# A decoder block on one core: first adaLN columns in two groups of 256, gates spread in one place, partial sums copied back into PSUM, another order of work

## The chip, the core and the metric

The kernel runs on one core of a Trainium2 chip. The time is device microseconds of one execution. The core has a matrix engine (TensorE, PE in the profile, with weight loads as PEld), a vector engine (VectorE, DVE), a scalar engine (ScalarE, ACT), GpSimd (POOL), and SyncE (SP), which here only issues DMAs. Each engine works through its own list of instructions in order and waits on semaphores for the others.

## What is computed

One layer of a hybrid decoder, 256 tokens of width 2048, in float32. Cut to what matters:

```python
mod = jax.nn.silu(c) @ w_ada[l] + b_ada[l]
sh1, sc1, g1, sh2, sc2, g2 = jnp.split(mod, 6, axis=-1)
h = modulate(rms_norm(x, norm1_g[l]), sh1, sc1)
proj = h @ w_in[l]
q, k, v, gb, gc, xt = jnp.split(proj, ...)
attn = moba_attention(q, k, v)
conv = gb * causal_dwconv(gc * xt, conv_w[l], conv_b[l])
mixed = jnp.concatenate([rms_norm(attn, attn_out_g[l]), rms_norm(conv, conv_out_g[l])], axis=-1)
x = x + g1[:, None, :] * (mixed @ w_out[l])
h2 = modulate(rms_norm(x, norm2_g[l]), sh2, sc2)
u = causal_dwconv(h2 @ w_ffn_up[l], ffn_conv_w[l], ffn_conv_b[l])
u_gate, u_up = jnp.split(u, 2, axis=-1)
x = x + g2[:, None, :] * ((jax.nn.silu(u_gate) * u_up) @ w_ffn_down[l])
```

`modulate(h, shift, scale)` is `h * (1 + scale) + shift`. With 256 tokens the attention has one block of keys and is plain causal attention over 8 heads of 128. Six vectors of 2048 (shift, scale and gate, twice) come out of the adaLN product of one row `c` with a matrix of 2048 by 12288.

## The kernel before

**Matrices.** Every large product splits its weights into two float32r parts, `hi` (a ScalarE copy, L640) and `lo` (the rest, a subtraction on VectorE or GpSimd, L649), and does the same with the activations. The input and output projections (`mm_tok`, L869 to L871) run three matmuls of 128x512 per block: hi by hi, lo by hi, hi by lo. A weight tile arrives as 512 KB in one of 10 buffers called `raw`; `lo` frees it and the next load is issued.

**Turns.** The program is a list of turns (slots in the code). The 49 turns of the input projection take four blocks of 128x512 each (the first three turns three, three and two); then come 16 turns of the output projection, then the FFN, up in matmuls called `z` (L1201, L1205), down in `mm_tok`. The six outputs have two halves each (q0, q1, k0 and so on); `turns` in the table CFG says which half is fed with which rows in which order. Consecutive turns of one half stay in two PSUM banks; when another half must have the banks, `evac_in` copies the sum out to SBUF (`pa_`, ScalarE, L881) or adds it there (VectorE, L883). What stands in the turn's loop is written into the engines' lists in that order: hi of the turn after next, tasks due in this turn, lo, adaLN steps, more tasks, then the matmuls of the turn.

**AdaLN.** A group is a stretch of columns of one of the six vectors. `ada` lists groups as part (0 shift 1, 1 scale 1, 2 gate 1, 3 shift 2, 4 scale 2, 5 gate 2), first block of 128, width, whether TensorE does it, first turn and span. On TensorE (L708) each 128 rows of the matrix are one matmul with 32 columns of weights, and four of them sit side by side in the array. On VectorE each 128 rows are one multiply-add with a column of `silu(c)` (L725). The numbers under `pre`, `mid` and `carry` say how many of these steps VectorE does at three places of a turn and how many it may leave. Then `evac` copies a TensorE group to SBUF, and `cols` (transposes, `adac`, and a sum, `adaz`) turns it into the columns A1 and B1 of `h = x*A1 + B1`, which `h_chunks` writes. A gate goes another way: `spread` (L786 to L799) sums the partitions with ones on TensorE into one row per quarter (`adab`), adds the bias, writes the row to DRAM, and `broadcast` reads it back to all partitions. The groups of gate 1 are spread one by one, and so are those of gate 2.

**The start** is written by hand. Blocks 0 and 1 of shift and scale are four TensorE groups of 128 columns; `x` is scaled (`xr`), transposed (`xn`) and copied out (`xnT`); turn 0 runs after block 0, turn 1 after block 1. Small vectors (`v`, `vf`: gains, conv weights) come over GpSimd's queue and are transposed into columns by `ffn_cols` (`pv_`, L575).

**The order around it.** `at` puts a task into a turn, `move` in CFG shifts a task by turns and within the turn, `pool` says per turn which of the two lo pieces go to GpSimd (1 first, 2 second, 3 both), `hi_late` whether hi comes after the first tasks.

Of the kernel before, what the change touches and what calls it, by code (L numbers as in the profile page):

```python
# [8 lines left out]
F32 = mybir.dt.float32  # L9
# [5 lines left out]
P = 128  # L15
# [16 lines left out]
CFG = {'ada': [[1, 2, 256, True, 0, 3], [0, 2, 256, True, 0, 3], [1, 4, 512, False, 2, 7], [0, 4, 512, True, 5, 4],  # L32
# [5 lines left out]
 'bufs': [41, 14, 10, 6, 2],  # L38
# [9 lines left out]
 'pre': {1: 0,  # L48
         2: 2,
         3: 0,  # L50
         4: 3,
         5: 3,
         6: 3,
         7: 2,
         9: 2,
         10: 4,
         11: 2,
         12: 2,
         13: 3,
         14: 0,  # L60
         15: 0,
         16: 2,
         17: 3,
         18: 4,
         20: 2,
         22: 0,
         23: 2,
         24: 0,
         27: 2,
         29: 0,  # L70
         30: 2,
         34: 3,
         36: 2,
         38: 2,
         39: 3,
         40: 4,
         42: 4,
         44: 0,
         46: 2,
         48: 2,  # L80
         51: 0,
         52: 3,
         54: 2,
         56: 3,
         57: 0,
         58: 2,
         61: 4,
         62: 4,
         63: 3,
         64: 3,  # L90
         65: 3,
         67: 4,
         69: 0,
         70: 0,
         74: 2,
         76: 3,
         77: 4,
         80: 0,
         83: 2,
# [4 lines left out]
         93: 0,  # L104
         95: 2,
         96: 3,
         97: 2,
         101: 2,
         103: 2,
         107: 3,  # L110
         112: 4,
         117: 3,
# [16 lines left out]
 'mid': {0: 4, 2: 4, 47: 1, 1: 4, 100: 1, 75: 0, 94: 3, 52: 0, 50: 1, 92: 4, 6: 3, 63: 0, 159: 2, 54: 0, 58: 2},  # L129
 'pool': {4: 1,  # L130
          5: 3,
          6: 3,
          9: 1,
# [8 lines left out]
          18: 3,  # L142
# [3 lines left out]
          22: 3,  # L146
          23: 3,
          24: 3,
          26: 3,
          27: 3,  # L150
          29: 3,
          31: 3,
          32: 3,
          33: 3,
          34: 3,
          35: 3,
          37: 3,
          38: 3,
          39: 3,
          2: 1,  # L160
          3: 2,
          40: 3,
          41: 1,
          48: 3,
          58: 0,
          49: 1,
# [4 lines left out]
          62: 2},  # L171
 'pool_h': [2, 3, 4, 5, 6, 7, 8, 9, 10, 11, 12, 13, 14, 15],
 'psum': [[0, 39]],
 'carry': {0: 2,
           1: 2,
           2: 2,
           4: 6,
           6: 1,
           9: 4,
           10: 3,  # L180
           12: 4,
           13: 4,
           14: 2,
           18: 4,
           21: 2,
           22: 1,
           30: 2,
           32: 6,
           34: 2,
           35: 4,  # L190
           36: 4,
           37: 4,
           38: 4,
           39: 3,
           43: 4,
           45: 6,
           46: 6,
           49: 2,
           50: 2,
           51: 3,  # L200
           52: 3,
           54: 3,
           55: 3,
           56: 3,
           57: 4,
           58: 4,
           59: 3,
           60: 4,
           61: 1,
           62: 3,  # L210
           63: 4,
           64: 4,
           65: 1,
           66: 2,
           67: 1,
           69: 3,
           72: 1,
           73: 2,
           74: 4,
           76: 2,  # L220
           79: 1,
# [22 lines left out]
           150: 2,  # L244
           159: 4,
# [1489 lines left out]
```

## Time and profile before

| what | value |
|---|---|
| median of 3 runs | 1183.02 us (1182.31 to 1183.23) |
| the profiled execution | 1182.27 us |
| its span in the trace | 1180.5 us |
| granted TensorE clock | 0.999 |
| instructions on TensorE, VectorE, ScalarE, GpSimd | 6045, 1305, 1015, 111 |
| read from HBM | 314.87 MB, 270 GB/s over the span |
| first projection matmul | 19.81 us |
| first FFN matmul | 441.83 us |
| hi pieces on ScalarE | 401 |
| lo pieces on VectorE, on GpSimd | 334, 67 |

A row of the profile names the line, the engine, the operation, the tile written and the tiles read. Matmuls overlap in the pipe, so the duration of one is longer than the distance to the next; rates are taken from the distance. Idle time of an engine counts only if the end of the program waits for it.

### The profile page before, as it was taken

Reading aid. Unit: us, or ns where it says so; the run is one execution under the profiler, and the core shown is the slowest. Engines: PE = TensorE matmul, PEld = TensorE weight load, DVE = VectorE, ACT = ScalarE, POOL = GpSimd, SP = SyncE. Lnnn points to the kernel's source line nnn. Section 1 sums busy time; section 2 is a strip of 40 time slices with the busy share of each in tenths; the row PEclk is TensorE's granted clock in tenths of the full one; section 3 lists DMA queues with packets and bytes.
Section 4 is the critical chain, followed back from the end, with each engine's and each line's share of the span. In section 5 each row is a group of like instructions: output and inputs, shape, how many; then the busy total and the mean of one; then the engine's idle time right before and its main releaser. Section 6 shows DMA issues by size and latency. Waiting matters only on the chain.

```text
span 1180.5 us, 17260 instructions
## 1 busy us (share of the span) xinstructions
PE 1156.3 (98%) x6045; PEld 964.4 (82%) x6045; DVE 916.4 (78%) x1305; ACT 638.6 (54%) x1015; POOL 184.6 (16%) x111
## 2 busy tenths in 40 slices
PE   5999999999999999999999999999999999999998
PEld 4668787788777868888888888888888888888886
DVE  3578988877688979999999644769867888665885
ACT  4664454568666545557675445555435455444561
POOL 2549895660100000000000000000000000000000
PEclk9999999999999999999999999999999999999999
DMA  9999999994699989996556755568896867885541
GB/s 332 385 409 366 407 404 357 392 380 144 211 342 360 336 270 360 364 319 214 175 180 201 237 171 179 175 218 266 290 326 200 307 232 248 262 258 178 166 156 71
DMA packets 211335, 320.23 MB, mean 271 GB/s; under 512 B 13624, under 2 KB 116204, under 8 KB 211248
## 3 DMA queue, kind: packets, MB, share of 16 engines
q1 hardware_dynamic: 208144, 314.62, 77.1%
q10 hardware_dynamic: 2496, 4.28, 1.1%
q8 instruction: 47, 0.77, 0.3%
q14 instruction: 40, 0.33, 0.1%
q0 software_dynamic: 608, 0.23, 0.1%
HBM read 314.87 MB, written 4.21 MB: 270 GB/s over the span
## 4 chain that ended last, share of the span: by engine, by line
PE 93%; DMA 4%; DVE 2%; ACT 1%; POOL 1%; issue 0%; DVEq 0%; ACTq 0%; POOLq 0%
PE z L1201 27%; PE z L1205 14%; DMA raw<-in_w_ada_dram 2%; PE ada L708 2%; DMA raw<-in_w_in_dram 1%; PE mq L871 1%; PE mk L869 1%; PE mq L869 1%; PE mq L870 1%; PE mk L870 1%; PE mk L871 1%; PE mv L869 1%; PE mg L869 1%; PE mg L870 1%; PE mg L871 1%; PE mv L871 1%
## 5 line engine op out<-in xcount | busy, mean ns | idle before, releaser
L640 ACT ACTIVATE hi<-raw 128x1024 fp32r<-128x1024 f32 (+1 forms) x401 | 401.3, 1031 | 341.1 <-PE z L1201 87.6
L649 DVE TENSOR_TENSOR lo<-raw,hi 128x1024 fp32r<-128x1024 f32 x334 | 388.9, 1204 | 106.5 <-ACT hi L640 97.6
L1201 PE MATMUL z<-h,hi 128*128 128x512 f32 x1408 | 328.8, 390 | 1.2 <-DVE h L1098 1.2
L1201 PEld LDWEIGHTS z<-h,hi 128*128 128x128 f32 x1408 | 261.3, 188 | 54.3 <-issue 2.0
L649 POOL TENSOR_TENSOR lo<-raw,hi 128x1024 fp32r<-128x1024 f32 x67 | 160.6, 2417 | 221.7 <-ACT hi L640 194.0
L725 DVE SCALAR_TENSOR_TENSOR ada<-raw,csil,ada 128x512 f32<-128x512 f32 (+1 forms) x201 | 184.9, 922 | 6.5 <-DMA raw<-in_w_ada_dram 1.8
L1205 PEld LDWEIGHTS z<-h,lo 128*128 128x128 f32 x1408 | 174.8, 192 | 3.4
L1205 PE MATMUL z<-h,lo 128*128 128x256 f32 x1408 | 176.0, 283 | 0.0
L1117 DVE TENSOR_TENSOR ub<-z,ub 128x256 f32<-128x256 f32 x120 | 43.5, 418 | 30.6 <-ACT ub L1114 30.4
L786 POOL MEMSET gb<- 128x512 f32 x2 | 1.1, 525 | 403.4 <-DVE uy L1140 403.4
L1114 ACT ACTIVATE ub<-z 128x256 f32<-128x256 f32 x120 | 39.2, 382 | 32.2 <-PE z L1201 32.2
L1133 ACT ACTIVATE uy<-ub,fc,fc 128x256 f32<-128x256 f32 x88 | 45.5, 592 | 0.1
L1140 DVE SCALAR_TENSOR_TENSOR uy<-ub,fc,uy 128x254 f32<-128x254 f32 x88 | 42.5, 483 | 3.1
L1138 DVE SCALAR_TENSOR_TENSOR uy<-ub,fc,uy 128x255 f32<-128x255 f32 x88 | 42.1, 479 | 0.4 <-ACT uy L1133 0.3
L1149 ACT ACTIVATE gh<-uy 128x512 fp32r<-128x512 f32 x22 | 13.8, 629 | 41.3 <-DVE uy L1147 41.2
L1143 ACT ACTIVATE uy<-uy 128x512 f32<-128x512 f32 x22 | 13.9, 633 | 34.9 <-DVE uy L1140 34.9
L708 PE MATMUL ada<-raw,crep 128*32 128x128 f32 (+2 forms) x320 | 27.7, 457 | 4.9 <-DMA raw<-in_w_ada_dram 4.7
L1150 DVE TENSOR_TENSOR gl<-uy,gh 128x512 fp32r<-128x512 f32 x22 | 15.2, 693 | 17.9 <-ACT gh L1149 17.9
L869 PE MATMUL mq<-hi,h 128*128 128x512 f32 x64 | 25.9, 404 | 0.9 <-ACT h L1279 0.9
L869 PE MATMUL mx<-hi,h 128*128 128x512 f32 x64 | 25.6, 400 | 0.0
L869 PE MATMUL mv<-hi,h 128*128 128x512 f32 x64 | 25.4, 397 | 0.1
L869 PE MATMUL mc<-hi,h 128*128 128x512 f32 x64 | 25.4, 397 | 0.0
(564 smaller groups left out, 1930.2 us busy)
## 6 DMA issues: line engine op xcount, KB each, us to landing
raw<-in_w_ada_dram SPq DMA_DIRECT2D x192, 512.0 KB, 7.0
raw<-in_w_ffn_up_dram SPq DMA_DIRECT2D x352, 256.0 KB, 4.7
raw<-in_w_in_dram SPq DMA_DIRECT2D x95, 512.0 KB, 7.8
raw<-in_w_ffn_down_dram SPq DMA_DIRECT2D x76, 512.0 KB, 5.1
raw<-in_w_out_dram SPq DMA_DIRECT2D x32, 512.0 KB, 7.2
raw<-in_w_ffn_down_dram SPq DMA_DIRECT2D x24, 256.0 KB, 3.6
xr<-in_x_dram SPq DMA_DIRECT2D x4, 512.0 KB, 4.6
gB<-gr ACTq DMA_DIRECT2D x8, 256.0 KB, 3.9
```

The costliest lines, as they stand in the source:

```text
L640: act(piece(his, "hi")[:, :m], t[:, :m], AF.Copy)
L649: (nc.gpsimd if pool in (i + 1, 3) else V).tensor_tensor(out=piece(los, "lo")[:, :m], in0=t[:, :m], in1=hi[:, :m].bitcast(F32), op=ALU.sub ...
L708: mm(self.acc[0][q:q + 32, :], crep[:, i, :], t, start=(r == 0 and j < 4), stop=(r == self.tiles - 1 and j >= self.rows - 4), tile_positio ...
L725: V.scalar_tensor_tensor(out=self.acc[n], in0=v, scalar=csil[:, i:i + 1], in1=acc, op0=ALU.mult, op1=ALU.add)
L869: mm(o, a, hi[k], start=(first and k == 0), stop=False)
L871: mm(o, b, hi[k], start=False, stop=(last and k == nk - 1))
L1117: V.tensor_tensor(out=d, in0=zp[grp][ft][:, :256], in1=d, op=ALU.add)
L1133: act(y, b, AF.Identity, bias=fcols[3][:, i:i + 1], scale=fcols[2][:, i:i + 1])
L1138: V.scalar_tensor_tensor(out=y[:, 1:], in0=b[:, :255], scalar=fcols[1][:, i:i + 1], in1=y[:, 1:], op0=ALU.mult, op1=ALU.add)
L1140: V.scalar_tensor_tensor(out=y[:, 2:], in0=b[:, :254], scalar=fcols[0][:, i:i + 1], in1=y[:, 2:], op0=ALU.mult, op1=ALU.add)
L1201: mm(zp[grp][ft], blk(hi, j)[:, ft * P:(ft + 1) * P], h2T[k + j], start=k + j == ks[0], stop=k + j == ks[1] - 1)
L1205: mm(zp[grp][ft][:, :256], blk(lo, j)[:, ft * P:(ft + 1) * P], h2T[k + j][:, :256], start=False, stop=False)
```

## The change

The edits, with the lists that set the order:

- the four groups of 128 columns at the start become two of 256 (scale, shift); turns 0 and 1 run in six parts that the list `start` orders, and the start's loads follow that list
- shift 1, columns 256 to 511, goes from TensorE to VectorE; gate 1's first two groups become one of 1024 columns
- `spread` runs once per gate, after its last group, over all four quarters
- `seed` copies a partial sum back into PSUM with ScalarE, the matmuls add to it, and `evac_in` copies the total out with ScalarE. The table lists seven names (half and number of its group). With the new order of turns, four of them name a group that exists: k0 1, k1 2, k1 3, x0 1
- at most two halves, not three, may share PSUM between a half's turns (`between`)
- the small vectors come over SP's queue in turn 7 and become columns in one bank in turn 14
- `lo_late`: the lo pieces of the last turn but one before the FFN come after the first steps of norm 2
- seven conv tiles of the mixed output skip the copy `my`; q0's squares are taken 512 wide and summed on VectorE
- the tables `turns`, `pre`, `mid`, `pool`, `carry`, `move`, `hi_late` are new, and `after` gives VectorE adaLN steps behind named tasks

```diff
-CFG = {'ada': [[1, 2, 256, True, 0, 3], [0, 2, 256, True, 0, 3], [1, 4, 512, False, 2, 7], [0, 4, 512, True, 5, 4],
+CFG = {'ada': [[1, 2, 256, True, 0, 3], [0, 2, 256, False, 0, 4], [1, 4, 512, False, 2, 8], [0, 4, 512, True, 4, 5],
...
-         [2, 0, 512, False, 23, 4], [2, 4, 512, False, 27, 4], [2, 8, 512, False, 31, 3], [2, 12, 512, False, 34, 4],
+         [2, 0, 1024, False, 23, 8], [2, 8, 512, False, 32, 2], [2, 12, 512, False, 34, 4],
...
- 'between': 3,
+ 'seed': ['c0 3', 'c1 3', 'k0 1', 'k1 2', 'k1 3', 'q1 3', 'x0 1'],
+ 'between': 2,
...
+ 'wide_sq': ['q0'],
+ 'fused': [8, 9, 10, 12, 13, 14, 15],
...
+    def seed(f, n):
+        assert f not in whole
+        whole[f] = None
+        mainp[f] = [bank(f"m{f}{t}", keep=True, seed=True) for t in range(2)]
+        for t in range(2):
+            act(mainp[f][t], pacc[f, t], AF.Copy)
...
-            if (f, t) not in pacc:
-                pacc[f, t] = t2k(f"pa_{f}{t}")
+            if (f, t) not in pacc or seeded[0]:
+                if not seeded[0]:
+                    pacc[f, t] = t2k(f"pa_{f}{t}")
                 act(pacc[f, t], p, AF.Copy)
             else:
                 V.tensor_tensor(out=pacc[f, t], in0=p, in1=pacc[f, t], op=ALU.add)
...
+            p = bank(f"adab{part}", full=False)
+            for q in range(4):
+                g = next(g for g in gates[part] if g.c0 <= 4 * q < g.c0 + g.nch)
+                assert g.out
+                flush(g)
+                x = (4 * q - g.c0) * P
+                mm(p[32 * q:32 * q + 32, :], (c32 if g.pe else ones)[:, :32],
+                   g.acc[x // g.w][:, x % g.w:x % g.w + 512],
+                   start=True, stop=True, tile_position=(0, 32 * q))
+            V.tensor_tensor(out=gs, in0=p, in1=gb, op=ALU.add)
...
-    ada_init = [Ada(part, k, P, True) for k in range(2) for part in (SC1, SH1)]
+    ada_init = [Ada(part, 0, 2 * P, True) for part in (SC1, SH1)]
...
+        if k in CFG["fused"]:
+            act(q, src, AF.Square)
+            act(mixT[k][:, :256], src, AF.Copy, scale=gcol)
+            V.scalar_tensor_tensor(out=mixT[k][:, 256:], in0=src, scalar=gcol, in1=mixT[k][:, :256].bitcast(F32),
+                                   op0=ALU.mult, op1=ALU.subtract)
+            return q
...
+        vecs.extend(rows(f"v{k}", v, nc.sync) for k, v in enumerate(srcs))
```

TensorE's list at the start, before. `ada_0_0` are the first groups, `adac` their column sums, `xn` transposes of x, `mq` the first projection matmuls:

```order
L708 MATMUL ada_0_0_160<-raw,crep 32x128 x16
L1599 MATMUL xn_183<-ident,xr 128x128 x4
L759 MATMUL adac_0_190<-ones,adae_0_181 128x1
L708 MATMUL ada_0_0_194<-raw,crep 32x128 x16
L759 MATMUL adac_0_217<-ones,adae_0_215 128x1
L1599 MATMUL xn_239<-ident,xr 128x128 x4
L1599 MATMUL xn_244<-ident,xr 128x128 x4
L869 MATMUL mq_249<-hi,h_225 128x512
```

The same place after the change:

```order
L1976 MATMUL xn_162<-ident,xr 128x128 x4
L979 MATMUL ada_0_0_167<-raw,crep 32x256 x16
L1034 MATMUL adac_0_194<-ident,adae_0_192 128x128 x2
L1976 MATMUL xn_201<-ident,xr 128x128 x4
L979 MATMUL ada_0_0_206<-raw,crep 32x256 x16
L1034 MATMUL adac_0_237<-ident,adae_0_235 128x128 x2
L1976 MATMUL xn_252<-ident,xr 128x128 x4
L1976 MATMUL xn_272<-ident,xr 128x128 x4
L1139 MATMUL mq_277<-hi,h_248 128x512
```

Both blocks of scale and of shift now stand ahead of the first projection matmul; before, the groups of block 1 stood between turns 0 and 1.

TensorE's list where the last group of gate 1 is spread, before (`at` are transposes of a head, `mx` a projection turn):

```order
L1368 MATMUL at_2597<-ident,pa_q_516 128x128
L1368 MATMUL at_2597<-ident,pa_k_488 128x128
L1368 MATMUL at_2597<-ident,pa_k_490 128x128
L795 MATMUL adab_12_2610<-adae_12_2530,ones 32x512
L869 MATMUL mx_2623<-hi,h_1372 128x512
```

And after:

```order
L1671 MATMUL at_2537<-ident,pa_k_439 128x128
L1065 MATMUL adab_2565<-adae_0_2069,ones 32x512
L1065 MATMUL adab_2565<-adae_0_2071,ones 32x512
L1065 MATMUL adab_2565<-adae_8_2243,ones 32x512
L1065 MATMUL adab_2565<-adae_12_2454,ones 32x512
L1139 MATMUL mx_2579<-hi,h_1389 128x512
```

The three earlier `adab` rows, each alone between two turns, came to this place.

SP's list of loads in turn 7, after the change (`raw` are weights of 512 KB, `v` the small vectors):

```order
L877 DMA raw<-in_w_in_dram 128x2x512 x4
L806 DMA v_753<-in_norm_g_dram 16x128
L806 DMA v_753<-in_conv_w_dram 24x128
L806 DMA v_753<-in_conv_b_dram 8x128
L806 DMA v_753<-in_attn_out_g_dram 8x128
L806 DMA v_753<-in_conv_out_g_dram 8x128
L806 DMA v_753<-in_q_norm_g_dram 1x128
L806 DMA v_753<-in_k_norm_g_dram 1x128
L806 DMA v_761<-in_ffn_conv_w_dram 88x128
L806 DMA v_763<-in_ffn_conv_w_dram 88x128
L806 DMA v_765<-in_ffn_conv_w_dram 88x128
L806 DMA v_767<-in_ffn_conv_b_dram 88x128
```

Before, these eleven stood at the head of GpSimd's list, ahead of its first lo piece. Behind them now come the next weights. GpSimd's list holds 55 lo pieces after and 67 before; the twelve stand in VectorE's list.

More of the change, by code (lines that the diff above doesn't have):

```diff
@@ L244 @@
            150: 2,
+           156: 6,
            159: 4,
@@ L651, in split_lo, with lo_late @@
             load_next()
+        splits.append((his, los))
+        if now[0] == N_OUT - 1:
+            late.extend(lambda i=i: half(i) for i in range(len(ts)))
+            return
+        for i in range(len(ts)):
+            half(i)
             if i == 0:
                 steps_of(CFG["mid"].get(now[0], 0))
-        splits.append((his, los))
+    late = []
+    def lo_late(n):
+        for _ in range(n):
+            if late:
+                late.pop(0)()
     csil = const.tile([P, NK], F32, name="csil")
@@ L690, in start @@
             if self.psum:
-                self.banks = [bank(f"{what}_{i}", keep=True) for i in range(self.n // self.w)]
+                self.banks = [bank(f"{what}_{i}", keep=True, full=False if self.pe else None) for i in range(self.n // self.w)]
                 self.acc = [t[:, :self.w] for t in self.banks]
@@ L860, in mm_tok @@
     def mm_tok(key, hi, lo, kts, nk, first, last, by_t=False):
-        if first:
-            mainp[key] = [bank(f"m{key}{t}", keep=True) for t in range(2)]
+        seeded = key in whole and whole[key] is None
+        if first and not seeded:
+            mainp[key] = [bank(f"m{key}{t}", keep=True, full=True) for t in range(2)]
         whole[key] = last
@@ L965, in evac_c @@
         done.add(f"ev{f}")
-        for t in range(2):
+        for t in ts:
             y = t2k(f"z{f}{t}")
@@ L1307, in tile_block @@
         spread_loads(Ada(part, c0, n, pe, any(b <= a and a + span <= e for b, e in CFG["psum"])), a, span)
+    for part, gs in gates.items():
+        s = max(g.end for g in gs)
+        put(s + 2, CFG["cls"]["spread"], gs[0].spread)
+        for f in range(4):
+            at(s + 3, broadcast, part, f)
     by_slot = {}
@@ new lines, in pieces @@
+    def pieces(n, b):
+        nb = slots[n][1]
+        his, los, raw = parts.setdefault(n, ([], [], []))
+        assert (n, b, "p") not in begun and (b == 0 or (n, b - 1, "p") in begun)
+        begun.add((n, b, "p"))
+        if b % 2 == 0:
+            raw.append(take())
+            piece(his, "hi")
+            piece(los, "lo")
+        act(blk(his, b), blk(raw, b), AF.Copy)
+        V.tensor_tensor(out=blk(los, b), in0=blk(raw, b), in1=blk(his, b).bitcast(F32), op=ALU.subtract)
+        if b % 2 or b == nb - 1:
+            load_next()
@@ new lines, in tile_block @@
+    g1n, bcol = [], []
+    for tok in CFG["start"]:
+        w, *n = tok.split()
+        n = [int(v) for v in n]
+        if w == "sA":
+            scale(0, 256)
+        elif w == "sB":
+            scale(256, 1024)
+        elif w == "sC":
+            scale(1024, 2048)
+        elif w == "vbc":
+            v = to_cols(vb, nb, "vbc")
+            g1n.append(v[:, 0:16])
+            bcol.append(v[:, 16:112])
+        elif w == "tr":
+            xn_tr(*n)
+        elif w == "out":
+            xn_out(*n)
+        elif w == "p":
+            pieces(*n)
+        elif w == "slot":
+            slot(*n)
+        elif w == "h":
+            h_chunks(n)
+        elif w == "warm":
+            warm(*n)
+        elif w == "go":
+            assert (*n, "p") in begun and (n[0], n[1] - 1) in begun or n[1] == 0
+            slots[n[0]][2](*parts[n[0]][:2], only=n[1])
+            begun.add(tuple(n))
+        elif w in by_name:
+            by_name[w].consume(*n)
+        elif w[-1] == "e":
+            by_name[w[:2]].evac()
+        else:
+            by_name[w[:2]].cols()
+        begun.add(w)
```

973 lines of the change are left out of this document (604 added, 369 removed), and 33 rows, old and new, of the table CFG.

## The prediction

> **What bounds the kernel now.** I read the engine shares first, then the stretches.
>
> ```profile
> span 1180.5 us, 17260 instructions
> PE 1156.3 (98%) x6045; PEld 964.4 (82%) x6045; DVE 916.4 (78%) x1305; ACT 638.6 (54%) x1015; POOL 184.6 (16%) x111
> ```
>
> TensorE leaves 24.2 us of the span idle. The table by stretches (length; then busy time of PE, PEld, DVE, ACT, POOL; granted clock, DMA share, GB/s) says where:
>
> ```profile
> 0.00:50.00 50.00, 34.74 (x306) 25.70 (x307) 21.32 (x49) 25.69 (x44) 15.48 (x24) 1.00 1.02 349
> 50.00:450.00 400.00, 396.03 (x1887) 312.27 (x1887) 327.38 (x493) 235.49 (x431) 166.62 (x83) 1.00 0.92 339
> 450.00:1160.00 710.00, 710.00 (x3787) 613.89 (x3786) 559.89 (x755) 375.32 (x539) 2.50 (x5) 1.00 0.71 234
> 1160.00:1180.50 20.50, 15.57 (x69) 12.58 (x67) 7.81 (x10) 2.12 (x2) 0.00 (x0) 0.97 0.13 51
> ```
>
> 15.3 us lie in the first 50, 4.0 in the next 400, none in the 710 of the FFN, 4.9 at the end. Is busy really working? The chain of waits (start, length, what):
>
> ```profile
> 461.54 7.28 PE z L1201 x32
> 468.82 1.91 PE z L1205 x16
> ```
>
> 32 matmuls of 512 columns in 7.28 us are 0.2275 us each, 256 columns take 0.119. The stream is dense: 1408 of the first and 1408 of the second make 489 us, the down projection's 1056 make 240, and the two fill 441.8 to 1171.5. So from about 43 us on time changes only with TensorE's own instructions or with new waits of TensorE. The waits it has between 50 and 434 us (engine, for whom; total, times, longest):
>
> ```profile
> PE adac L763 <- ACT adae L743: 0.9, 2, 0.7
> PE adac L763 <- DVE adae L725: 0.9, 1, 0.9
> ```
>
> **Part one: the start.** TensorE, rows of the first 45 us:
>
> ```profile
> 19.81 0.78 PE L869 MATMUL mq<-hi,h 128*128 128x512 f32 x1
> 20.39 0.63 PE L870 MATMUL mq<-lo,h 128*128 128x512 f32 x1
> 20.81 0.63 PE L871 MATMUL mq<-hi,h 128*128 128x512 f32 x1
> ...
> 34.16 1.04 PE L1599 MATMUL xn<-ident,xr 128*128 128x128 f32 x8
> ...
> 41.70 0.64 PE L708 MATMUL ada<-raw,crep 128*32 128x256 f32 x8 [0.72 <-DMA raw<-in_w_ada_dram]
> 42.27 0.28 PE L575 MATMUL pv_v1c<-ident,v 66*128 66x66 f32 x1
> ...
> 43.11 0.47 PE L869 MATMUL mk<-hi,h 128*128 128x512 f32 x1
> ```
>
> Turn 2 starts at 43.11, and what held it is a load: the last adaLN rows for TensorE landed at 41.70. By the order of the loads, that is the 26th half megabyte. After the change shift columns 256 to 511 go to VectorE, so the last load TensorE needs ahead of turn 2 is the 25th. The rate there:
>
> ```profile
> 10.00:20.00 10.00, 7.54 (x81) 5.93 (x82) 4.49 (x17) 5.47 (x11) 0.25 (x1) 1.00 1.12 361
> ...
> 30.00:40.00 10.00, 9.09 (x82) 6.05 (x80) 4.86 (x7) 5.00 (x9) 2.23 (x1) 1.00 1.04 374
> ```
>
> 0.524 MB at 374 GB/s are 1.4 us. The column transposes (42.27 to 43.0) also move out of this place, behind turn 14: 0.7. Turn 2 starts near 41.0, **2.1 us earlier**. The price inside: before the first projection matmul, 12 loads must land and not 8. Four loads at 361 GB/s are 5.8 us, so mq moves from 19.81 to about 26. This is covered: behind it stand 36 matmuls (8.2 us), about 1.2 us for slow first ones (0.42 apart at 20.39 and 20.81, six of them), two such blocks of transposes as at 34.16 (2.1) and the first half of the adaLN rows (1.0), to 38.5, which is 1.8 us before the 25th load. Past 27.8 each microsecond of delay would count in full. The 64 narrow adaLN matmuls become 32 of double width: the same columns, before turn 2, so nothing on the sum.
>
> **Part two: the gates.**
>
> ```profile
> 193.07 0.98 PE adab L795 x2
> ...
> 258.12 0.97 PE adab L795 x2
> ...
> 871.11 0.98 PE adab L795 x4
> ```
>
> One quarter costs 0.98 us, two quarters side by side also 0.98. Four such places for G1 become one, two for G2 become one. If four quarters go like two, 3 x 0.98 + 0.98 = 3.9 us less TensorE time; if they run as two pairs, 1.96 less for G1 and nothing for G2. I take the first, since doubling from one to two cost nothing. [...]
>
> **Part three: the bridge into the FFN.**
>
> ```profile
> 409.97 0.87 PE x1t L1021 x8
> ...
> 441.83 1.38 PE L1201 MATMUL z<-h,hi 128*128 128x512 f32 x5 [1.15 <-DVE h L1098]
> ```
>
> One 0.87 us block of transposes leaves the dense stretch and goes behind the last adaLN matmuls, where TensorE waits 1.15 us for h: **0.9 us less**, hidden by that wait. The chain of norm 2 itself keeps its steps.
>
> **Part four: VectorE, ScalarE, GpSimd.** Rows per group (busy, mean ns | idle before):
>
> ```profile
> L649 DVE TENSOR_TENSOR lo<-raw,hi 128x1024 fp32r<-128x1024 f32 x310 | 374.2, 1244 | 103.0 <-ACT hi L640 94.1 <-PE z L1205 6.0 <-DMA raw<-in_w_ffn_up_dram 1.3
> L883 DVE TENSOR_TENSOR pa_k<-mk,pa_k 128x512 f32<-128x512 f32 x12 | 7.8, 681 | 3.3 <-PE mk L871 3.3
> L1093 DVE SCALAR_TENSOR_TENSOR h2f<-x1T,A,n2b 128x256 f32<-128x256 f32 x8 | 3.7, 476 | 1.2 <-ACT rB L1077 1.2
> L799 DVE TENSOR_TENSOR gs<-adab,gb 32x512 f32<-32x512 f32 x4 | 2.7, 685 | 4.1 <-PE adab L795 4.0
> L881 ACT ACTIVATE pa_k<-mk 128x512 f32<-128x512 f32 x4 | 2.1, 588 | 0.0
> ```
>
> Up to the gate's sum VectorE does 30 lo pieces and not 15 (+18.3 at 1.22), 10 adds less (-6.8), three gate sums less (-2.1), and 16 adaLN steps of 256 columns more (+7.0 to 7.7): about **+16 us**. Its room:
>
> ```profile
> 45.00:258.00 213.00, 211.91 (x947) 167.37 (x945) 174.54 (x243) 114.33 (x198) 156.50 (x79) 1.00 1.03 388
> ```
>
> 174.5 of 213 become about 191 of 209. That is 82% to 91%: room is left, but waits of VectorE reach TensorE more often. The 0.9 us wait above came from it. I let the two waits (1.8) grow by two thirds: **+1.2**, with ends of -1.8 (both vanish) and the slow rival below. ScalarE's copies back into PSUM do not occur in the trace; the copy out takes 0.588, a copy from SBUF to SBUF is near it, so between 0.5 and 0.7 each. Only four of the seven listed sums exist as groups (k0 1, k1 2, k1 3, x0 1): 8 copies, 4.7 us on an engine with 99 us of room in this stretch. If one came late it would hold a TensorE group for up to 0.6. I take nothing. Seven conv tiles lose one ScalarE pass; two wide squares replace eight narrow ones: both off TensorE, nothing.
>
> **Part five: eleven small loads on SP's queue.**
>
> ```profile
> vf<-in_ffn_conv_w_dram POOLq DMA_DIRECT2D x3, 44.0 KB, 5.1
> vb<-in_norm_g_dram ACTq DMA_DIRECT2D x1, 8.0 KB, 4.8
> 0.74 1.80 SPq L1561 DMA_DIRECT2D xr<-in_x_dram  x4
> ```
>
> They move from GpSimd's queue at the start into SP's at turn 7 (some 70 us). Eight loads are in flight at a time, by the waits in the program, so these eleven push the weights out of the pipe: four issues of 0.45 while nothing large flies, and then some of the 4.8 to 5.1 us that a load needs to land. Bounds: nothing, if the lead covers it, to 4.5 us. Weights land about 10 us ahead of their matmuls there (22.5 MB moved at 62 us, used at 74; an estimate from the GB/s of the stretches), less some 4 for hi and lo. I take **+1.0**.
>
> Sum: -2.1 + 0.7 (the column transposes come later) - 3.9 - 0.9 + 1.2 + 1.0 = **-4.0 us**. The profiled execution took 1182.27, its span 1180.5; the median of the runs is 1183.02, 0.75 above it. 1182.27 - 4.0 = 1178.3; I say 1178.5.
>
> **Rivals.** *The gain stays whole.* VectorE at 91% still never holds TensorE, the lead covers the small loads: -6.2, and the two old waits may go too: 1174.3 to 1176.1. For it: DVE is never longer than its stretch. Against: it was already the waited-for engine at 82%.
>
> *The loads give it back.* Two stretches of the loads:
>
> ```profile
> 60.00:70.00 10.00, 10.00 (x46) 6.76 (x45) 7.43 (x8) 8.14 (x14) 3.55 (x3) 1.00 1.04 414
> ...
> 90.00:100.00 10.00, 10.00 (x46) 8.29 (x45) 8.44 (x12) 7.97 (x12) 9.74 (x8) 1.00 0.95 333
> ```
>
> From 45 to 258 us DMA moves 388 GB/s on the mean, of the 414 it reaches at best; a TensorE that asks 2 to 5 us earlier, and a gap of 4.5 in the pipe, leave no lead. Then TensorE follows the loads up to the attention: gates of G1 and start are lost, G2 and the bridge stay, and half of the gap shows: 1182.27 - 1.9 + 1.5 = 1182. Against: the rate fell to 333 between 90 and 100 us while TensorE was full, so there is slack to catch up.
>
> *VectorE becomes the bound; slower.* Lo pieces take turns with GpSimd's:
>
> ```profile
> L649 POOL TENSOR_TENSOR lo<-raw,hi x24: 2377/2406/2417, 44.6 to 128.8; 128x1024 fp32r<-128x1024 f32 x24
> L649 DVE TENSOR_TENSOR lo<-raw,hi x6: 1211/1950/2830, 45.9 to 78.9; 128x1024 fp32r<-128x1024 f32 x6
> ...
> 37.77 5.69 POOL L649 TENSOR_TENSOR lo<-raw,hi 128x1024 fp32r<-128x1024 f32 x2 [27.52 <-DMA raw<-in_w_ada_dram]
> 38.67 2.57 DVE L649 TENSOR_TENSOR lo<-raw,hi 128x1024 fp32r<-128x1024 f32 x1 [1.29 <-ACT hi L640]
> ```
>
> While GpSimd ran two of them from 37.77 to 43.46 (5.69 for 2 x 2.4), VectorE's piece took 2.57 and not 1.22. With 30 pieces at a mean m, VectorE's time in the stretch is 174.5 + 16 - 4.4 (what the six long ones hold already) + 30 (m - 1.22). It passes 209 at m = 1.98, close to the median of 1.95 in the row; at m = 2.35 it is 220, TensorE ends 11 later, net +5: 1187.5. It decides from m = 2.2 on. Against: GpSimd does 12 pieces less, and most of the newly split turns give VectorE the first half, so it starts first. [...]
>
> *It does not do what it says.* Four sums and not seven go through PSUM. This costs the forecast nothing, since it priced four.
>
> **How the numbers follow.** Forecast (1176.1 to 1180.6) 0.48; whole gain 0.20; given back by the loads 0.18; VectorE the bound 0.14. The range reaches from the whole gain with both old waits gone and 1 us more at the start (1173.0) to the given-back case with 2 us for the open bounds (1184.0); outside stay most of the last rival and a little below. About 0.2% can be told from no change: faster below 1180.65 holds forecast and whole gain, 0.68; the given-back case and a little of the slow one are the same, 0.20; slower 0.12.
>
> **What would show it.** Right: turn 2 (mc) starts near 41; one place with four adab of about 1 us near 250 us and one near 985; the first z about 2 to 4 us before 441.8; PE full from there. Wrong: mq later than 28; adab at 2 us; PE idle of more than 3 us between 50 and 434, waiting for DVE (the slow rival) or with DMA at the head of ACT's waits around 75 to 115 us (the loads); lo on DVE at a mean above 2 us before 258.

## The result, and the profile after

| kernel | median | fastest to slowest | executions |
|---|---|---|---|
| before | 1183.07 us | 1182.31 to 1183.23 | 4 |
| changed | 1177.16 us | 1175.53 to 1178.23 | 4 |

The ratio is 0.995, 95% interval 0.9937 to 0.9963: 4.4 to 7.5 us faster. The profiled execution took 1178.11 us, 4.16 less than the profiled one of before; the sum of the forecast was 4.0. The total was right, and several of its terms were not.

The page of the changed kernel (span 1176.3 us), engines:

```profile
PE 1147.9 (98%) x5945; PEld 958.8 (82%) x5945; DVE 926.6 (79%) x1316; ACT 642.0 (55%) x1008; POOL 152.4 (13%) x88
```

The same by stretches:

```profile
0.00:50.00 50.00, 30.95 (x205) 21.07 (x206) 24.71 (x50) 23.80 (x40) 7.50 (x12) 1.00 0.95 343
50.00:450.00 400.00, 395.28 (x1901) 313.51 (x1900) 337.98 (x510) 242.07 (x432) 140.16 (x72) 1.00 0.94 344
450.00:1160.00 710.00, 710.00 (x3793) 614.88 (x3792) 558.13 (x750) 376.14 (x537) 4.72 (x6) 1.00 0.70 232
```

TensorE is idle for 4.7 us between 50 and 450, more than the 4.0 before. The gain is not idle time saved: the FFN is as dense as it was. What has gone is TensorE's own work, and some of that gain was paid back in new waits. Four places of its timeline:

```profile
41.18 0.50 PE L1139 MATMUL mc<-hi,h 128*128 128x512 f32 x1 [2.08 <-ACT pa_q L1159]
...
258.27 1.06 PE L1065 MATMUL adab<-adae,ones 128*32 128x512 f32 x8
259.26 0.50 PE L1139 MATMUL mx<-hi,h 128*128 128x512 f32 x1
...
439.11 3.94 PE L1490 MATMUL z<-h,hi 128*128 128x512 f32 x16
...
983.55 1.06 PE L1065 MATMUL adab<-ada,ones 128*32 128x512 f32 x8
984.54 0.50 PE L1139 MATMUL m('D', 2, 0)0_9742<-hi,gh 128*128 128x512 f32 x1
```

Four quarters of a gate take 0.99 us (258.27 to 259.26, 983.55 to 984.54), as long as one quarter did (0.97 in the kernel before, 258.05 to 259.02). What a place takes out of the stream is a little more than its row. One of the three that are gone, in the kernel before (`adab` itself starts at 193.00):

```profile
192.68 0.39 PE L871 MATMUL mk<-hi,h 128*128 128x512 f32 x1
...
193.98 0.50 PE L869 MATMUL mk<-hi,h 128*128 128x512 f32 x1
194.31 0.39 PE L870 MATMUL mk<-lo,h 128*128 128x512 f32 x1
```

From 192.68 to 194.31 pass 1.63 us, where two distances of 0.2275 would be 0.45: the place costs 1.18.

Turn 2 starts at 41.18, where 41.0 was forecast. But the wait in brackets ends with ScalarE's copy of q's sum, not with a load. The five longest of its waits from there to the bridge (engine, for whom; total, times, longest):

```profile
PE mc L1139 <- ACT pa_q L1159: 2.1, 1, 2.1
PE mx L1139 <- ACT pa_c L1159: 1.2, 1, 1.2
PE mk L1139 <- ACT mk L1148: 0.9, 1, 0.9
PE mv L1139 <- ACT pa_k L1159: 0.6, 1, 0.6
PE mc L1140 <- POOL lo L906: 0.6, 1, 0.6
```

Three of the five are ScalarE's copies out of PSUM; `mk` at L1148 is a partial sum on its way back in, an operation that the trace of before did not have. VectorE, to which the forecast gave its 1.2 us, ends only two of the three shorter ones, 0.3 each.

ScalarE's list at the start of turn 2 shows the new order:

```profile
36.76 3.88 ACT L895 ACTIVATE hi<-raw 128x1024 fp32r<-128x1024 f32 x4
40.55 2.05 ACT L1159 ACTIVATE pa_q<-mq 128x512 f32<-128x512 f32 x4
...
48.66 1.06 ACT L895 ACTIVATE hi<-raw 128x1024 fp32r<-128x1024 f32 x1 [3.87 <-DMA raw<-in_w_in_dram]
...
51.12 1.07 ACT L1159 ACTIVATE pa_c<-mc 128x512 f32<-128x512 f32 x2
```

Four hi pieces stand ahead of the first copy; and at 48.66 a hi piece waits 3.87 us for a load while the copy that TensorE needs for `mx` (51.12) stands behind it. Why is that load late? The longest of SyncE's waits between 28 and 45 us, and the stretch with its DMA share and GB/s:

```profile
SPq L877 <- PE ada L979: 6.3, 1, 6.3
```

```profile
37.50:40.00 2.50, 1.60 (x32) 0.69 (x24) 1.22 (x3) 2.50 (x4) 2.11 (x1) 1.00 0.37 74
```

The queue of loads stood 6.3 us for a buffer full of adaLN rows that TensorE came to only at 37.16. DMA fell to 74 GB/s, a hole that the start before did not have (374 GB/s there between 30 and 40).

### The profile page after: what moved, and what is told of

Read it like the earlier page. It is cut to its first block, busy times and chain, and to the rows that moved or that the text cites. A ratio compares the mean times of both kernels' runs of the same rounds, so it can differ in the third digit from the quotient of the medians.

```text
span 1176.3 us, 17016 instructions
## 1 busy us (share of the span) xinstructions
PE 1147.9 (98%) x5945; PEld 958.8 (82%) x5945; DVE 926.6 (79%) x1316; ACT 642.0 (55%) x1008; POOL 152.4 (13%) x88
## 4 chain that ended last, share of the span: by engine, by line
PE 82%; DMA 6%; DVE 5%; POOL 2%; issue 2%; ACT 2%; SPq 0%; ACTq 0%; POOLq 0%; DVEq 0%
PE z L1490 27%; PE z L1494 14%; DMA raw<-in_w_in_dram 5%; POOL lo L906 2%; DVE ada L996 2%; DMA raw<-in_w_ada_dram 2%; PE ada L979 2%; ACT hi L895 1%; PE mx L1139 1%; PE mg L1139 1%; PE mx L1141 1%; PE mg L1141 1%; PE mg L1140 1%; PE mx L1140 1%; PE mv L1139 1%
## 5 line engine op out<-in xcount | busy, mean ns | idle before, releaser
L906 DVE TENSOR_TENSOR lo<-raw,hi 128x1024 fp32r<-128x1024 f32 x346 | 404.8, 1207 | 107.5 <-ACT hi L895 100.6
L996 DVE SCALAR_TENSOR_TENSOR ada<-raw,csil,ada 128x512 f32<-128x512 f32 (+2 forms) x215 | 189.0, 891 | 5.9 <-DMA raw<-in_w_ada_dram 2.2
L906 POOL TENSOR_TENSOR lo<-raw,hi 128x1024 fp32r<-128x1024 f32 x55 | 135.5, 2487 | 298.9 <-ACT hi L895 263.3
L1422 ACT ACTIVATE uy<-ub,vcols 128x256 f32<-128x256 f32 x88 | 45.5, 594 | 0.1
L1429 DVE SCALAR_TENSOR_TENSOR uy<-ub,vcols,uy 128x254 f32<-128x254 f32 x88 | 42.5, 483 | 3.1
L1427 DVE SCALAR_TENSOR_TENSOR uy<-ub,vcols,uy 128x255 f32<-128x255 f32 x88 | 42.0, 478 | 0.3 <-ACT uy L1422 0.2
L1139 PE MATMUL mk<-hi,h 128*128 128x512 f32 x64 | 25.4, 396 | 0.9 <-ACT mk L1148 0.9
L1139 PE MATMUL mg<-hi,h 128*128 128x512 f32 x64 | 25.7, 402 | 0.0
```

The lines of the kernel that those rows point to most:

```text
L906: (nc.gpsimd if pool in (i + 1, 3) else V).tensor_tensor(out=piece(los, "lo")[:, :m], in0=t[:, :m], in1=hi[:, :m].bitcast(F32), op=ALU.sub ...
L996: V.scalar_tensor_tensor(out=self.acc[n], in0=v, scalar=csil[:, i:i + 1], in1=acc, op0=ALU.mult, op1=ALU.add)
L1139: mm(o, a, hi[k], start=(first and k == 0 and not seeded), stop=False, skip_group_check=True)
L1422: act(y, b, AF.Identity, bias=fcols[3][:, i:i + 1], scale=fcols[2][:, i:i + 1])
L1427: V.scalar_tensor_tensor(out=y[:, 1:], in0=b[:, :255], scalar=fcols[1][:, i:i + 1], in1=y[:, 1:], op0=ALU.mult, op1=ALU.add)
L1429: V.scalar_tensor_tensor(out=y[:, 2:], in0=b[:, :254], scalar=fcols[0][:, i:i + 1], in1=y[:, 2:], op0=ALU.mult, op1=ALU.add)
```

## The experiments

All times are medians; differences are against the kernel before on the same chip, in the same group of runs. The changed kernel, measured so, is 4.3 (second chip) to 5.9 us faster.

**The changed kernel again.**

> The changed kernel once more, unchanged: the measure for the other runs of this group, and a second profile. Both theories expect 1175 to 1178.5 us. In the profile, theory A (the waits that are new are fixed by the order of instructions) expects the same new waits of TensorE at the same places and sizes: 0.86 for k1's partial sum at 216, 0.61 for pa_k at 239, 1.22 for pa_c at 51.8, and turn 2 at 41.2. Theory B (they follow the arrival of loads, which differs from run to run) expects places that move: the 2.7 us between the fastest and the slowest run shows in the start or in waits behind a hi piece that waits for a load.

1177.83 us, before 1182.16; ratio 0.9962 (0.9949 to 0.9976). Its profiled execution took 1176.12, and TensorE's waits from 40 to 434 us were:

```profile
PE mx L1139 <- ACT pa_c L1159: 1.8, 1, 1.8
PE mc L1139 <- ACT pa_q L1159: 1.7, 1, 1.7
PE mk L1139 <- ACT pa_c L1159: 0.7, 1, 0.7
PE mc L1140 <- POOL lo L906: 0.6, 1, 0.6
PE mk L1139 <- ACT mk L1148: 0.5, 1, 0.5
PE as L1682 <- DVE adae L996: 0.3, 1, 0.3
```

Each theory holds in part. The waits for q's copy, for `pa_c` and for the partial sum are there in both executions, with other sizes; the one for `pa_k` at 239 and that for GpSimd at 180 are gone. From 60 us to the bridge TensorE waited 0.7 us here and 2.1 in the first profile. The 2 us between two executions of one program lie there. Turn 2 starts 0.6 us earlier here (40.54), but that is gone at 59.7, where both are level (`adac` at 59.75 in the first, at 59.74 here); it comes from the places at 165, 180, 216 and 239. Ahead of the waits at 180 and 239 ScalarE had waited for loads (0.95 and 2.73 us, in the first profile); the one at 216 hangs on VectorE's add.

**Without the partial sums put back**, and the same with the adaLN steps that hang on these tasks kept:

```diff
- 'seed': ['c0 3', 'c1 3', 'k0 1', 'k1 2', 'k1 3', 'q1 3', 'x0 1'],
+ 'seed': [],
```

> The list of sums put back into PSUM is emptied: ScalarE loses 8 copies in and 8 copies out, VectorE gets 8 adds of 0.68 us back. The forecast priced the copies at nothing: no change, within 0.5 us of the changed kernel. Theory A, from the wait of 0.86 at 216 where the copy into mk waits for VectorE's add of pa_k: 0.9 us less. Rival: the 5.4 us more on VectorE between 60 and 258 come back as waits of TensorE for lo pieces or adaLN rows: 1 to 3 us more.

```diff
     def seed(f, n):
         assert f not in whole
-        whole[f] = None
-        mainp[f] = [bank(f"m{f}{t}", keep=True, seed=True) for t in range(2)]
-        for t in range(2):
-            act(mainp[f][t], pacc[f, t], AF.Copy)
...
-                    (group[f] > 0 and f"{f} {group[f]}" in CFG["seed"],))
+                    (False,))
```

> The changed kernel with the four partial sums added by VectorE again, as in the run with the empty list, but with the adaLN steps that hang on the names of these tasks kept in their places, so that only 8 adds of 0.68 us are added to VectorE's list (and 16 copies leave ScalarE's). If VectorE's time itself is the price (5.4 us more where TensorE waits for it), the run is still 4 to 7 us slower than the changed kernel, with waits of TensorE for pa_k, pa_x and pa_v. If the 7.4 us came from the adaLN steps that lost their place (the wait of 1.8 for the last adae of a group at 88), it is within 1.5 us of the changed kernel. The forecast, which gave the copies no price, expects no difference.

1185.25 us, 7.4 more than the changed kernel beside it and 3.1 more than before (ratio 1.0027, 1.0017 to 1.0038). With the steps kept: 1185.86, 3.3 more than before (1.0028, 1.0018 to 1.0038). So lost steps are not the cause; VectorE's adds are: with the steps kept TensorE waits at the same places (pa_v 3.9 us, adae 1.8, pa_x 1.2). TensorE's waits from 60 to 434 us in the first of the two:

```profile
PE mk L1139 <- DVE pa_v L1161: 3.0, 1, 3.0
PE mx L1139 <- DVE adae L996: 1.8, 1, 1.8
PE mc L1139 <- DVE pa_x L1161: 1.1, 1, 1.1
PE mv L1139 <- DVE pa_k L1161: 0.4, 1, 0.4
```

Eight adds of 0.68 us became 6.8 us of waits in all (2.1 in the changed kernel). And two of the waits cost more than their length. TensorE around them, with its matmuls in the second column and the granted clock in the third from the end:

```profile
87.50:90.00 2.50, 1.72 (x7) 1.46 (x8) 1.93 (x3) 0.60 (x2) 2.50 (x2) 0.95 0.49 107
90.00:92.50 2.50, 2.50 (x7) 1.92 (x7) 0.00 (x0) 0.00 (x0) 0.99 (x1) 0.50 0.98 355
92.50:95.00 2.50, 2.50 (x11) 2.00 (x10) 0.00 (x0) 0.69 (x1) 0.00 (x0) 0.87 1.06 408
...
222.50:225.00 2.50, 1.50 (x4) 1.25 (x5) 2.46 (x5) 1.77 (x2) 1.60 (x1) 0.58 1.05 408
225.00:227.50 2.50, 2.50 (x10) 2.01 (x9) 2.39 (x4) 0.00 (x0) 2.50 (x2) 0.74 1.05 407
```

After the wait of 1.8 at 88 TensorE was granted half its clock from 90 to 92.5, and 7 matmuls stand in a stretch that has 12 or 13 at full clock. Clock lost times length is 1.7 us at each place, of which some 0.3 at the second fall into the wait itself. The 4.7 us of longer waits and these 3.4, less 0.5 for an earlier turn 2, give 7.6; against the first profile of the changed kernel z moved by 7.8 (446.91 for 439.11).

**Gates one by one in the changed kernel**, twice. The second attempt loads the bias once and keeps the last group's place in its turn:

```diff
-            for q in range(4):
-                g = next(g for g in gates[part] if g.c0 <= 4 * q < g.c0 + g.nch)
+            for q in mine:
+                g = self
...
-        put(s + 2, CFG["cls"]["spread"], gs[0].spread)
+        for g in gs:
+            put(g.end + (4 if part == G1 and g is not gs[-1] else 2), CFG["cls"]["spread"], g.spread)
```

> The gates are spread group by group again, at three places for gate 1 and two for gate 2 (five places of adab in place of two). If four quarters side by side cost as much as one (rows of 0.98 us), three more places are 3 x 0.98 = 2.9 us more. If two pairs ran in turn and a single place were cheaper: 1 us more or less. Rival: the places lie beside waits that absorb them (0.6 to 0.9 us each near 216 and 239): 1 to 2 us more.

> The changed kernel with its gates spread group by group, as before the change: the bias of a gate is loaded once, and the last group is spread at the same place of its turn as in the changed kernel, which the first attempt did not keep. Three more places of 0.98 us: 2.9 us more than the changed kernel. Rival from the first attempt (22 us more): the sum of a group on VectorE waits for the bias on GpSimd's queue and holds VectorE, and with it TensorE: 5 us or more, with DVE waiting for gb or adab in the trace.

1199.63 and 1196.41 us: 17.5 and 15.5 more than before. Both miss the 2.9 us by far. ScalarE, VectorE and TensorE in the second, near 236:

```profile
236.10 0.72 ACTq L1077 DMA_DIRECT2D gr<-gs  x2
236.94 2.00 ACT L896 ACTIVATE hi<-raw 128x1024 fp32r<-128x1024 f32 x2 [5.71 <-DVE ada L995]
238.85 1.06 ACT L1165 ACTIVATE pa_k<-mk 128x512 f32<-128x512 f32 x2
```

```profile
235.38 0.68 DVE L1074 TENSOR_TENSOR gs<-adab,gb 64x512 f32<-64x512 f32 x1 [2.09 <-DMA gb<-in_b_ada_dram]
```

```profile
239.48 0.80 PE L1145 MATMUL mc<-hi,h 128*128 128x512 f32 x1 [5.76 <-ACT pa_k L1165]
```

The gate's sum waits for the bias; the rows of the gate leave on ScalarE's queue and wait for the sum; ScalarE stands 5.7 us with its hi pieces and the copy of `pa_k` behind them; TensorE waits 5.8. A wait of 6.1 us at 266, for the last adaLN step of the group that is spread last, and the clock behind both (0.94 granted from 200 to 260 us, 0.98 from 260 to 440) add to it. This measures a bad place, not the price of three spreads. For that the change was made alone, from the other side:

**Before, with each gate spread in one place, and nothing else.** In this kernel and in the two of the last experiment the second quarter of gate 2 takes the values of the fourth; instructions and sizes are as described.

```diff
+            gates.setdefault(self.part, []).append(self)
+            if self.c0 + self.nch < NK:
+                return
+            p = bank(f"adab{self.part}")
+            for q in range(4):
+                g = next(g for g in gates[self.part] if g.c0 <= 4 * q < g.c0 + g.nch)
```

> The kernel before with one part of the change alone: each gate is spread in one place, after its last group, all four quarters side by side (four places of adab become one for gate 1, two become one for gate 2; the gate's bias is still loaded at the turn of the first group). The forecast's step: 3 x 0.98 + 0.98 = 3.9 us less than before. Rival: TensorE in front of the attention is held by loads, so that the 2.9 us of gate 1 come back as waits there and only gate 2's 0.98, in the dense FFN, stays: 1 us less. In the profile: z in the first case 2.9 earlier than 441.8, in the second at 441.8.

1177.48 us, 5.0 less than before (ratio 0.9957, 0.9945 to 0.9969): the whole gain of the change from one of its nine parts. TensorE, at the spread, and the waits between 50 and 434 us:

```profile
253.95 1.07 PE L797 MATMUL adab<-adae,ones 128*32 128x512 f32 x8
...
437.50 3.91 PE L1202 MATMUL z<-h,hi 128*128 128x512 f32 x16 [1.14 <-DVE h L1099]
```

```profile
PE adac L761 <- ACT adae L741: 0.9, 2, 0.7
```

The block starts 4.1 us ahead of the last one before (258.05 there). Three places of 1.18 make 3.5 of it, and the loads did not take them back. The rest is not the gates': the wait of 0.9 for VectorE at 126 us, 67 us ahead of the first place, is not in this profile, and with its restart it is worth 1.0. A later kernel with the gates in one place still waits 0.6 there. On the other side this execution was granted 0.61 of the clock from 42.5 to 45 us and 0.71 from 45 to 47.5, with the start as before the change: 1.7 us lost, of which 0.6 are still missing at 65 (`mg` at 65.64 for 65.03). Four places of 1.18 are 4.7, near the 5.0 of the medians.

The places cost the other engines too: in the kernel before, ScalarE had this wait between 180 and 300 us, which is gone here. TensorE did not wait behind it:

```profile
ACT hi L640 <- DMA gr<-gs: 6.0, 1, 6.0
```

**Transposes of x1 back in the dense stretch.**

```diff
-          'tr_out 1': (2, 0),
-          'tr_out 2': (3, 1),
+          'tr_out 1': (-1, 1),
+          'tr_out 2': (3, -2),
```

> The transposes of two parts of x1 go back to where they stood before the change: one block at 415 inside the output projection, the other ahead of norm 2, none behind the last adaLN matmuls. The forecast's step: the first FFN matmul waits for h again, about 0.9 us, and the run is 0.9 us longer. Rival: norm 2's own chain (n2d on VectorE, then h) is what ends last, and it starts when the last output turn ends; then the block put ahead of it delays it all the same and the run is 0.9 to 1.8 longer. Second rival: the block was hidden in both orders: within 0.3 us.

1178.24 us, 0.4 more than the changed kernel beside it; the intervals overlap (0.9968, 0.9955 to 0.998), so the times don't settle it. The trace shows the step itself: z waits for h again.

```profile
PE z L1490 <- DVE h L1385: 1.1, 1, 1.1
```

From the last block of the output projection to z pass 7.57 us (432.09 to 439.66) and 7.48 in the changed kernel (431.63 to 439.11): as long in the changed kernel with a block of transposes more in it. So the wait hides the block, as forecast. That the whole run gains the block's 0.9 us is not shown; z starts 0.55 earlier in the changed kernel.

**Small loads early again.**

```diff
-        vecs.extend(rows(f"v{k}", v, nc.sync) for k, v in enumerate(srcs))
+        vecs.extend(rows(f"v{k}", v, nc.gpsimd) for k, v in enumerate(srcs))
...
+    load_v_()
```

> The eleven small loads go back to the head of GpSimd's queue; nothing else moves. In the changed kernel they let DMA fall to 75 to 90 GB/s from 85 to 90 us, about 1.6 MB or 4 us of loading lost, and TensorE did not wait there. The forecast: 1.0 us less without them. Theory A (the lead covers the hole for good): no difference, within 0.4. Theory B (the hole is paid later, where ScalarE's hi pieces wait for loads and hold the copies behind them: pa_k at 239, lo at 180): 0.5 to 1.0 less, and the waits of TensorE at 180 and 239 are gone. Against both: the loads collide with the first ones at the start, as before the change: up to 0.5 us more there.

1179.22 us, 3.3 less than before (0.9963, 0.995 to 0.9977): no faster than the changed kernel. The hole in the loads, in the changed kernel and then in this one:

```profile
85.00:87.50 2.50, 2.50 (x12) 2.07 (x12) 2.43 (x5) 2.15 (x3) 1.79 (x1) 1.00 0.25 90
87.50:90.00 2.50, 2.50 (x12) 2.07 (x12) 0.63 (x2) 1.23 (x3) 2.50 (x2) 1.00 0.29 75
```

```profile
85.00:87.50 2.50, 2.50 (x13) 2.06 (x11) 2.39 (x4) 1.50 (x2) 0.71 (x1) 1.00 1.05 406
87.50:90.00 2.50, 2.50 (x13) 2.07 (x12) 1.71 (x3) 1.92 (x4) 2.50 (x2) 1.00 1.05 408
```

The hole was real, of the size expected (some 4 us of loading), and TensorE stayed full across it. The partial sum's wait near 216 was even longer without it (1.5). This profile also lost 1.7 us of clock behind a wait of 2.0 at 52.6 (0.66 granted from 52.5 to 57.5 us), so its time alone settles nothing below that. The term of 1.0 is nothing that could be measured.

**Shift on TensorE again.**

```diff
-CFG = {'ada': [[1, 2, 256, True, 0, 3], [0, 2, 256, False, 0, 4],
+CFG = {'ada': [[1, 2, 256, True, 0, 3], [0, 2, 256, True, 0, 3],
```

> Shift 1, columns 256 to 511, goes back to TensorE (16 matmuls with 32 columns of weights more, about 1 us; VectorE loses 16 steps of 256 columns, 7 us). The forecast's step: turn 2 waits for one more half megabyte, 1.4 us later than 41. Rival, from the profile after: turn 2 waits for ScalarE, which has four hi pieces (3.9 us) ahead of the first copy of q's sum, and not for a load; then it costs about the 1 us of matmuls or less, and VectorE's 7 us return as shorter waits: within 1 us of the changed kernel, either side.

1181.06 us, 1.5 less than before (0.9984, 0.9975 to 0.9994), so by the two ratios 2.6 us of the gain are lost: more than either expectation, though the two intervals just overlap. Its profiled execution was its fastest but one (1178.62). There TensorE waited 1.21 and 0.77 us for the added loads, and the clock fell behind them:

```profile
40.00:42.50 2.50, 0.75 (x12) 0.27 (x16) 2.50 (x2) 2.50 (x7) 2.50 (x1) 0.88 1.01 353
42.50:45.00 2.50, 2.50 (x12) 1.41 (x13) 1.58 (x1) 0.66 (x3) 0.50 (x1) 0.50 1.01 345
45.00:47.50 2.50, 2.50 (x8) 1.94 (x7) 1.57 (x2) 1.17 (x2) 0.00 (x0) 0.50 1.06 410
47.50:50.00 2.50, 2.50 (x10) 2.01 (x9) 2.39 (x4) 0.48 (x1) 0.00 (x0) 0.75 1.02 406
```

Those rows lose 3.4 us. Between 50 and 434 its waits are only 1.2 us. So the move of the shift to VectorE seems to buy a safer start and to pay for it in later waits. No profile shows one of the slower executions of this kernel (to 1182.92). But the mean granted clock was taken in every execution: 0.996 to 0.998 in all twelve, 0.998 or 0.999 in the five of the changed kernel run again, and 0.001 of the run is 1.2 us.

**Turn 2 earlier still.**

```diff
-                put(i + 1, CFG["cls_evac"], evac_in, f, i == uses[f][-1],
+                put(i + (0 if (i, f) == (1, 'q0') else 1), CFG["cls_evac"], evac_in, f, i == uses[f][-1],
...
-          2: 3,
+          2: 2,
```

> The changed kernel with ScalarE's first two copies of q's sum ahead of two of the four hi pieces, and the first lo piece of turn 2 on VectorE in place of GpSimd. If turn 2 waits for ScalarE's order (the reading of the profile after), mc starts 1.0 to 1.5 us earlier (at 39.5 to 40) and its wait of 0.58 for GpSimd's lo goes; if the loads behind it are then late, the wait of 1.2 to 1.8 at 51.8 (pa_c behind a hi piece that waits for a load) grows by as much and the run is unchanged within 0.5 us; if they are not, 1 to 2 us less. If turn 2 waits for a load, mc stays at 40.5 to 41.2.

1176.51 us, 4.4 less than before (0.9965, 0.9953 to 0.9978): as the changed kernel. TensorE:

```profile
38.93 0.50 PE L1139 MATMUL mc<-hi,h 128*128 128x512 f32 x1 [0.20 <-ACT pa_q L1159]
41.04 0.50 PE L1140 MATMUL mc<-lo,h 128*128 128x512 f32 x1 [0.23 <-POOL lo L906]
51.48 0.50 PE L1139 MATMUL mx<-hi,h 128*128 128x512 f32 x1 [3.58 <-ACT pa_c L1159]
```

Turn 2 did wait for ScalarE's order: with the copies ahead it starts 2.2 us sooner than at 41.18. And `mx` stays at 51.5, where it was (51.75, 51.67 in the two profiles of the changed kernel): the wait for the load behind `pa_c` took all of it. At the start the loads set the pace.

**Before, with the gates and the bridge.** To the single spread comes the block of x1 behind the last adaLN matmuls; gate 1's rows wait in three buffers of their own, for which the general ones are two fewer. The second kernel also takes the buffers of bias and sum only at the place of the spread.

```diff
-          'tr_out 2': (3, -2),
+          'tr_out 2': (3, 1),
```

> The kernel before with two parts of the change: each gate spread in one place (the rows of gate 1 now kept in three buffers of their own, taken from the 41 general ones, until they are read), and the transposes of the third part of x1 behind the last adaLN matmuls. Order of the input projection, loads, VectorE's and GpSimd's shares are those of before. From the forecast's terms: 3.9 + 0.9 = 4.8 us less than before, and so as fast as the changed kernel or 0.5 faster: then the rest of the change (start, sums put back, shift on VectorE, lo pieces, small loads) adds nothing on balance. Rival: the rest is worth some of the gain, and this kernel stays 1 us or more behind the changed one (less than 4 us gained). Two buffers fewer may cost: a wait of TensorE that was not there before would show it.

> The kernel before with each gate spread in one place and the third part of x1 transposed behind the last adaLN matmuls, as in the run before last, but with the gate's bias and sum rows in buffers taken at the place of the spread, not eleven turns earlier. The order of everything else is that of before. If the gates and this block carry the whole gain of the change, it takes as long as the changed kernel: 4 to 5.5 us less than before. The rival: the bias, loaded by GpSimd only when it comes to that place, is late and holds the sum on VectorE, and the rows behind it on ScalarE's queue: 2 us or less gained, with VectorE waiting for gb near 250.

1177.17 us, 3.7 less than before (0.9968, 0.9955 to 0.998), and 1179.4, 3.3 less (0.9979, 0.997 to 0.9988). Both gain less than was expected (4.8, and 4 to 5.5). The first is as fast as the changed kernel within the intervals. In the second VectorE stood 4.0 us ahead of the gate's sum, and ScalarE 5.0 for the rows behind it. The bias is issued only at that place there; in the kernel before it took 4.3 us from issue to landing (median of eight). TensorE waited 1.5 us for VectorE's add of `pa_x` near 272, which fits the rival's mechanism, and its profile has a dip of the clock to 0.50 at 42.5 to 47.5, like the one above. No version was clearly faster than the changed kernel.

## Why the prediction was right, and where not

By its steps, from the two profiled executions:

| step | forecast | measured |
|---|---|---|
| turn 2 starts earlier | -2.1 | -1.9 |
| waits between it and 60 us | 0 | +2.1 |
| gate 1 in one place | -2.9 | -3.5 |
| column transposes later | +0.7 | +0.3 |
| x1's block into the bridge | -0.9 | -0.9 |
| waits from 60 to 434 us | +1.2 | +0.3 |
| gap of the small loads | +1.0 | 0 |
| first z | -3.0 | -2.7 |
| gate 2 in one place | -1.0 | -1.2 |

The column transposes take 0.3 at 114.3. Gate 1 is three places of 1.18. The measured rows down to the gap make -3.6; the 0.9 to z's -2.7 are about what restarts add to the waits. The wait of 0.58 at 43.65 takes 0.84 out of the stream (1.30 from 42.68 to 43.98, where two distances are 0.46). Five such waits at 0.26, less three of 0.16 in the kernel before, are 0.8 (an estimate from these rows). Gate 2's row is the shift of the first matmul behind it (984.54 for 988.45) less that of z. The rest of the 4.2 us is behind 985.

**The gates** are the gain. The mechanism held: four quarters took 0.99 us where one or two had taken 0.97 to 0.98, and the change alone on the kernel before confirms it end to end. The size was a fifth too small, since the forecast took the row of 0.98 for the cost of a place and left out the slower distances beside it (1.18 in all). What the step left out too is that a place also holds ScalarE, whose queue writes the rows: a hi piece waited 6.0 us for them at 200 us in the kernel before.

**The start: a right number from a wrong step.** The forecast said that the last load TensorE needs ahead of turn 2 is the 25th, and that it ends last. It did not: the rows were there at 37.16, and ScalarE's four hi pieces held the start to 41.18. And the 1.9 us were gone by 60. The price that the step named (mq later, 25.18 where about 26 was forecast) was covered as it said. Not seen was that TensorE, by coming later to the adaLN rows, holds buffers that the next loads need: SyncE stood 6.3 us. Of the rivals, "the loads give it back" is what happened, but for this part alone.

**The waits** were put on VectorE, whose busy time would rise by 16 to 191 of 209 us. Between 45 and 258 it is 180.8, up 6.3. There are 26 lo pieces on VectorE in this stretch and not 30, with a median of 1.22 us and a mean of 1.42; the longest, 3.27 from 174.17 on, ran beside seven pieces in a row on GpSimd (173.97 to 192.52). So the slow rival's condition (a mean from 2.2 us on) was far off. The two old waits and the new ones balance to +0.3 in one profile; in the other they are 1.0 less than before.

**The sums put back** were priced at nothing, as copies on an idle engine, with a wait of up to 0.6 if late. The wait exists: 0.5 to 0.9 us, where the copy stands behind VectorE's add and that behind 2.8 us of adaLN steps. What the pricing missed is what they replace: without them the kernel is 7.4 us slower, and slower than before. So the changed order needs them: in the kernel that adds on VectorE instead, the engine is busy for 181.0 of the 213 us from 45 to 258, 85%, and TensorE waits 6.8 us for its results between 60 and 434.

**The small loads**: the hole was sized rightly and the lead covered it. The term should have been nothing.

By these rows the start and the restarts cost 3.2 us more than forecast, and the gates, the column transposes, the later waits and the small loads 3.1 less. That these errors cancel is luck, and it is why the sum of 4.0 met 4.16. The experiments put it more simply: the gates alone gain 3.7 to 6.5 us by their interval, as much as the change gains, and no worth of all other parts together could be measured. The two kernels with the gates and the bridge (3.7 and 3.3 us) do not narrow that down.

## What to carry to other kernels

Count the matrix engine's own instructions in a dense stretch first: that term had its mechanism right and its size within a fifth, while every term for waits was off in sign or size. Take such a cost from the distance between the matmuls on both sides of it, not from its own row. When a start moves earlier, look for the next thing the loads gate: the gain ends there, and an engine that comes later to its data may hold the very buffers the loads need. An engine's busy share says little about what 5 us more on it cost (here 6.8 us of waits behind an engine at 85%); try it at the place where its results are waited for.

## What the runs showed of the hardware that was not expected

Some waits of TensorE cost more than their length. In the kernel without the sums 1.7 us of clock were lost behind each of two waits, of 1.8 and 3.0 us (0.50 granted from 90 to 92.5, 0.58 from 222.5 to 225). At the start of the kernel with shift on TensorE 3.4 us were lost behind a pair of 1.2 and 0.8 (0.50 granted from 42.5 to 47.5). The other dips of the experiments that were read in steps of 2.5 us lost 1.7 or 3.4 us each too, but for the longest. It goes with the wait of 9.0 us in the first kernel with gates one by one: 0.50 granted from 265 to 272.5 us and 0.81 from there to 275, 4.2 us lost in these rows.

The loss does not follow from the length of the wait. One of 1.81 at 88.28 brought a dip in the kernel without the sums, one of 1.82 at 88.64 brought none with the steps kept (1.00 granted from 70 to 110), and 3.58 at 51.5 in the kernel with the early turn 2 left the clock at 1.00 from 50 to 60. At the start a pair of 0.70 and 0.78 brought one in the kernel with the single spread (0.61 and 0.71 granted from 42.5 to 47.5), a pair of 0.75 and 0.72 none in the kernel before (1.00 granted from 37.5 to 62.5). What decides it was not tried.

This bears on the medians. In the group with the early turn 2, the four executions of the kernel before with a mean clock of 0.996 to 0.998 took 1181.27 to 1183.18 us, the five at 1.0 took 1179.98 to 1180.88. So part of a difference between medians can be how often each kernel met a dip; the experiments do not separate it. The kernel with the single spread had no advantage there: its five executions have 0.996 to 0.998.

The DMAs that write a gate's rows stand in ScalarE's list. In the second kernel with gates one by one they wait for a sum that is not ready (the ACTq row at 236.10); ScalarE stood 5.7 us ahead of the hi pieces behind them, and TensorE waited 5.8.
